# Softmax attention: three of four head pairs store their sums to DRAM and are normed later, with the head dims on partitions

## The chip, the cores and the metric

The kernel runs on one core of one Trainium2 chip. The metric is the device time of one execution in microseconds (us); the figure for a kernel is the median of its runs. A profile is one further execution, recorded by the hardware profiler.

## What is computed

A trunk of two layers over 1040 frames (16 learned meta frames and 1024 inputs) of 1024 features, in float32. Each layer norms its input, projects it, runs two head groups side by side (four heads of gated linear attention, GLA, and eight heads of softmax attention with a forget bias, FoX), norms each head, projects the concatenation back and adds it; then a gated feed-forward with a causal convolution. The part that matters here, cut from the reference:

```python
logits = jnp.einsum('bqhd,bkhd->bhqk', q_b, kf) + c_b[..., None] - c_k[:, :, None, :]
logits = jnp.where(key_pos[None, :] <= q_pos[:, None], logits, -jnp.inf)
o = jnp.einsum('bhqk,bkhd->bqhd', jax.nn.softmax(logits, axis=-1), vf)
...
o_fox = rms_norm(o_fox, fox_norm[i].reshape(FOX_HEADS, FOX_DH)).reshape(B, L, FOX_WIDTH)
h = h + jnp.concatenate([o_gla, o_fox], axis=-1) @ w_out[i]
```

A head has 64 dims. With s the unnormalised sum of exp(logit) v and z the sum of exp(logit), the softmax output is s / z, and its RMS norm is s / sqrt(mean(s^2) + EPS z^2): the denominator never divides, it only enters the norm as EPS z^2. Both kernels use this form (64 EPS z^2 beside the sum of squares over 64 dims).

## The kernel before, in words

Everything is kept with features on the 128 partitions and frames along the free dim. A float32 product is made of three passes in a faster float format: an operand is split into a rounded part and the rest, hi and lo, and `mm3` (L252 to L258) issues hi x hi, lo x hi and hi x lo. `split` (L369) makes the two parts with a cast on ScalarE (ACT, L372) and a subtraction on VectorE (DVE, L373).

In each layer the GLA heads run first, then the FoX stage (`fox`, L823), then the output projection and the feed-forward. The FoX stage treats the eight heads as four pairs p (two heads e of 64 dims fill 128 partitions) and the 1040 query frames as nine tiles of 116 frames (the first has 112), in five groups g of tiles: (7, 8), (5, 6), (3, 4), (1, 2), (0,). One step, or slot, is one tile of one head: 18 slots for a pair, 72 for a layer, eight more to drain.

A step n does the following, and a table `due` holds what follows in later slots:

- `fox_scores` (L697): two matmuls for each chunk of up to 464 keys into a PSUM tile of tag S (three buffers), bias and minimum on DVE (L715), the exponential on ACT (L727), which also sums the row; the row sums are gathered in `den` (L731), queries on partitions.
- slot n+2: the probabilities P are transposed on TensorE (PE, L748) and split into PT.
- slot n+3: `fox_av` (L752). PT is the moving operand; the stationary one holds V's hi part in 64 columns and its lo part in the other 64. So the result `av` (PSUM, one buffer) has the 64 head dims twice on the partitions, the sum with V hi and the sum with V lo, and the frames along the free dim. ACT copies it to SBUF (L777, `avs`).
- slot n+4, after head 1 of a group: `fox_fold` (L779). Four PE transposes (two for the single-tile group) turn `avs` so that frames lie on partitions (L787); ACT copies the hi part (L790), DVE adds the lo part (L791); ACT squares (L793), DVE sums over the 64 dims (L797), adds 64 EPS z^2 (L795, L798), and `rsqrt` (L305 to L311) gives a factor for each frame and head, tiles of a few elements a row; DVE multiplies (L802).
- slot n+6: `fox_store` (L806). Two transposes (one) bring the dims back on partitions (L813). Pairs 0, 1 and 2 are scaled by the norm's gain on ACT (L820) and stored by a DMA issued on GpSimd (POOL, L821) in a DRAM tensor `mixd`; pair 3 is split at once into the operand of the output projection (L817).

Between these, `work.run` fills every slot with projection matmuls ("mm" in the profile; 24 for a chunk of about 348 frames): while a pair is under way, the projections of the next pair (`fox_products`, L607) and then those of a GLA output gate (`gr_products`, L664). A gate unit is evacuated with single buffers of tags ge and gy and one of the two buffers of tag vt, in a chain of DVE and ACT operations (L672 to L683), and the gated GLA head goes to `mixd` as well. The last plan (L1028) loads the last parts of `mixd` (L1031, POOL), splits all of them into the operand of the output projection (L1047) and starts that projection inside the FoX stage.

The order of the instructions on each engine is made from program order by priority (the scores stand eight higher, L871) and by when their inputs are expected. SP (SyncE) issues the weight loads (L214), the moves of k (L638), the bias rows cb (L863) and the loads of GLA heads for the gates (L669), in one queue.

## Time and profile before

| | us |
|---|---|
| median of 3 runs (lowest to highest) | 2478.85 (2476.86 to 2479.68) |
| the profiled execution, device time | 2479.26 |
| its span in the trace | 2477.3 |
| mean granted TensorE clock of it | 0.997 |

| engine | share of the span busy |
|---|---|
| PE (matmuls) | 99% |
| DVE | 76% |
| ACT | 53% |
| POOL | 16% |

In the lines of the profile "L787" is line 787 of the kernel, "out<-in" are the program's names, sizes are partitions x elements, and times are us unless marked ns. PEld is the loading of PE's stationary operand, which overlaps the matmuls; the ends of matmuls are modelled. In a line of busy time by stretch the first figures are the stretch and its length, then each engine's busy time with its number of instructions, then the granted clock, the busy share of the DMA engines and GB/s. In a row of a source line stand the count, then the least, median and longest duration in ns, then the first and last start.

### The profile page before, as it was taken

Reading aid. Unit: us, or ns where it says so; the run is one execution under the profiler, and the core shown is the slowest. Engines: PE = TensorE matmul, PEld = TensorE weight load, DVE = VectorE, ACT = ScalarE, POOL = GpSimd, SP = SyncE. Lnnn points to the kernel's source line nnn. Section 1 sums busy time; section 2 is a strip of 40 time slices with the busy share of each in tenths; the row PEclk is TensorE's granted clock in tenths of the full one; section 3 lists DMA queues with packets and bytes.
Section 4 is the critical chain, followed back from the end, with each engine's and each line's share of the span. In section 5 each row is a group of like instructions: output and inputs, shape, how many; then the busy total and the mean of one; then the engine's idle time right before and its main releaser. Section 6 shows DMA issues by size and latency. Waiting matters only on the chain.

```text
span 2477.3 us, 47313 instructions
## 1 busy us (share of the span) xinstructions
PE 2447.8 (99%) x18286; PEld 2365.1 (95%) x18286; DVE 1875.6 (76%) x3769; ACT 1321.2 (53%) x2857; POOL 384.0 (16%) x565
## 2 busy tenths in 40 slices
PE   9999999999999999999999999999999999999998
PEld 8999999999999999999999999999999999998887
DVE  7666776869988888865865666777699888887667
ACT  7345766646555555642643466666465555556433
POOL 2023433210000000100210234331100000001002
PEclk9999999999999999999999999999999999999999
DMA  4232134333322214764412222243423212247722
GB/s 135 73 84 75 43 95 130 125 125 102 120 75 81 88 68 143 197 153 136 128 41 75 77 79 73 68 146 108 148 82 111 91 65 90 82 149 180 214 72 87
DMA packets 121872, 261.00 MB, mean 105 GB/s; under 512 B 15136, under 2 KB 36896, under 8 KB 121648
## 3 DMA queue, kind: packets, MB, share of 16 engines
q1 hardware_dynamic: 97440, 182.81, 23.9%
q0 software_dynamic: 22336, 72.88, 10.4%
q8 instruction: 143, 2.34, 0.4%
q10 hardware_dynamic: 1872, 2.31, 0.3%
q14 instruction: 81, 0.66, 0.1%
HBM read 177.31 MB, written 67.85 MB: 99 GB/s over the span
## 4 chain that ended last, share of the span: by engine, by line
PE 66%; issue 16%; DVE 11%; ACT 4%; DMA 2%; POOL 1%; SPq 0%; DVEq 0%; POOLq 0%; ACTq 0%
PE mm L256 8%; PE mm L258 7%; PE mm L257 7%; PE up L257 5%; PE up L258 5%; PE up L256 5%; PE down L257 4%; PE down L256 4%; PE down L258 4%; PE av L774 3%; PE tr L748 2%; PE S L712 1%; ACT P L727 1%; DVE S L715 1%; PE S L713 1%
## 5 line engine op out<-in xcount | busy, mean ns | idle before, releaser
L257 PE MATMUL up<-x,lo 128*128 128x260 f32 x2240 | 632.9, 283 | 0.9 <-DVE lo L1156 0.8
L256 PE MATMUL up<-x,hi 128*128 128x260 f32 x2240 | 632.8, 283 | 0.1
L258 PE MATMUL up<-x,hi 128*128 128x260 f32 x2240 | 632.9, 283 | 0.0
L257 PEld LDWEIGHTS up<-x,lo 128*128 128x128 f32 x2240 | 421.7, 188 | 1.4 <-DVE lo L1156 1.3
L256 PEld LDWEIGHTS up<-x,hi 128*128 128x128 f32 x2240 | 421.6, 188 | 0.4 <-ACT hi L1155 0.3
L258 PEld LDWEIGHTS up<-x,hi 128*128 128x128 f32 x2240 | 421.9, 188 | 0.0
L1155 ACT CAST hi<-raw 128x512 fp32r<-128x512 f32 (+1 forms) x490 | 266.4, 553 | 209.2 <-PE up L258 90.9
L256 PE MATMUL mm<-xh,hi 128*128 128x348 f32 (+4 forms) x1056 | 362.0, 343 | 0.0
L1156 DVE TENSOR_TENSOR lo<-raw,hi 128x512 fp32r<-128x512 f32 (+1 forms) x490 | 286.8, 600 | 78.7 <-ACT hi L1155 78.0
L258 PE MATMUL mm<-xl,hi 128*128 128x348 f32 (+4 forms) x1056 | 340.6, 322 | 0.0
L257 PE MATMUL mm<-xh,lo 128*128 128x348 f32 (+4 forms) x1056 | 339.7, 322 | 0.0
L256 PEld LDWEIGHTS mm<-xh,hi 128*128 128x128 f32 x1056 | 200.5, 190 | 2.0 <-issue 1.4
L257 PEld LDWEIGHTS mm<-xh,lo 128*128 128x128 f32 x1056 | 200.4, 190 | 0.1
L258 PEld LDWEIGHTS mm<-xl,hi 128*128 128x128 f32 x1056 | 199.2, 189 | 0.1
L1137 DVE TENSOR_TENSOR raw<-raw,raw 128x512 f32<-128x512 f32 (+1 forms) x230 | 147.0, 648 | 32.4 <-DMA raw<-in_wd_dram 30.1
L727 ACT ACTIVATE P<-S,m 116x460 f32<-116x460 f32 (+2 forms) x224 | 125.1, 562 | 71.5 <-DVE m L715 68.4
L256 PE MATMUL down<-x,hi 128*128 128x260 f32 (+1 forms) x504 | 161.1, 320 | 0.7 <-DVE dg L1614 0.7
L257 PE MATMUL down<-x,lo 128*128 128x260 f32 (+1 forms) x504 | 161.2, 320 | 0.4 <-DVE lo L1156 0.4
L223 ACT CAST hi<-raw 128x512 fp32r<-128x512 f32 (+2 forms) x152 | 87.4, 576 | 138.4 <-PE mm L258 53.8
L258 PE MATMUL down<-x,hi 128*128 128x260 f32 (+1 forms) x504 | 161.1, 320 | 0.0
L373 DVE TENSOR_TENSOR PT<-tr,PT 116x464 fp32r<-116x464 f32 (+3 forms) x240 | 122.9, 515 | 48.8 <-ACT PT L372 47.3
L1416 POOL DMA_DIRECT2D actd<-cv x44 | 23.5, 535 | 736.9 <-DVE cv L1415 736.9
(313 smaller groups left out, 5960.5 us busy)
## 6 DMA issues: line engine op xcount, KB each, us to landing
raw<-in_wm_dram SPq DMA_DIRECT2D x330, 256.0 KB, 3.0
raw<-in_wd_dram SPq DMA_DIRECT2D x48, 256.0 KB, 4.7
actd<-cv POOLq DMA_DIRECT2D x22, 520.0 KB, 3.0
actd<-cv POOLq DMA_DIRECT2D x22, 512.0 KB, 3.1
cb<-cd SPq DMA_DIRECT2D x16, 520.0 KB, 4.2
hm<-h POOLq DMA_DIRECT2D x32, 260.0 KB, 3.7
kA<-kA SPq DMA_DIRECT2D x24, 260.0 KB, 4.2
kL<-kL SPq DMA_DIRECT2D x24, 260.0 KB, 4.8
```

The costliest lines, as they stand in the source:

```text
L223: nc.scalar.copy(hi[:, :n, :], raw[:, :n, :])
L256: nc.tensor.matmul(ps, wh, xh[:, c0:c0 + n], start=first, stop=False, skip_group_check=more)
L257: nc.tensor.matmul(ps, wl, xh[:, c0:c0 + n], start=False, stop=False, skip_group_check=more)
L258: nc.tensor.matmul(ps, wh, xl[:, c0:c0 + n], start=False, stop=last, skip_group_check=more)
L373: nc.vector.tensor_tensor(out=lo, in0=src, in1=hi.bitcast(F32), op=ALU.subtract)
L712: nc.tensor.matmul(S[:rows, :n], q["qA"][e][:, qs], q["kA"][e][:, c0:k1], start=True, stop=False)
L727: nc.scalar.activation(P[:rows, :n], S[:rows, :n], AF.Exp, scale=-1.0, bias=m[:rows, nch - 1:nch], accum_out=(den if nch == 1 else d3[:row ...
L748: nc.tensor.transpose(tr[:w, 3 - j, :rows], P[:rows, o:o + w], id_)
L774: nc.tensor.matmul(av[:, a:b], w.rearrange("p a b -> p (a b)"), x, start=(t == ts[0] and part == 0 and i == 0), stop=(t == last and i == 1))
L1137: nc.vector.tensor_tensor(out=q[out][:, :nk, :], in0=q[a][:, :nk, :], in1=q[b][:, :nk, :], op=op)
L1155: nc.scalar.copy(hi[:, :nk, :], src[:, :nk, :])
L1156: nc.vector.tensor_tensor(out=lo[:, :nk, :], in0=src[:, :nk, :], in1=hi[:, :nk, :].bitcast(F32), op=ALU.subtract)
```

## The change

For pairs 0, 1 and 2 the fold, its norm and the store are taken out. Pair 3 keeps them.

- `fox_av`: the hi and lo sums are on different partitions of `av`; ACT copies one of the two halves (64 partitions) over to the other's partitions, DVE adds the other half from PSUM. Head 0 ends on partitions 0 to 63, head 1 on 64 to 127. After head 1, POOL issues the store of the unnormed sums in `mixd`.
- `fox_den`: twice for each pair (groups 0 to 2, groups 3 and 4) the row sums, squared and scaled, are turned by one PE transpose so that they lie as rows; SP stores the rows in a small DRAM tensor. The row sums of a pair now live in one tile for all nine tiles of queries.
- `fox_load`: in slot n+12, 10, 8, 6 or 6 (by group) SP loads the sums of the group back and, for each head, the row of 64 EPS z^2, repeated on 64 partitions.
- `fox_square`, at the end of that slot: squares on ACT, split into hi and lo.
- `fox_norm`, one slot later: two matmuls with a block matrix of ones (64 x 64 blocks on the diagonal, `pair`) sum the squares over each head's 64 dims and repeat the sum on its 64 partitions; DVE adds the denominators; `rsqrt` runs on the full width (128 partitions x 232 frames); DVE multiplies sums, gain and factor in one operation; POOL issues the store in `mixd`.

The working tiles of the new steps use the tags of others: ge, gy and vt of the gate units and projections, ff and fon of the fold. `avs` is used for the single-tile group too. The diff, cut to its core:

```diff
+        self.dd = [(dp.tile([12, FT], F32, name=f"dd{p}"), dp.tile([6, FT], F32, name=f"de{p}")) for p in range(3)]
...
-        if last < 4 * part + 4:
+        if last < 4 * part + 4 and to is None:
             nc.scalar.copy(avs[:, e, :width], av[:, :width])
+        elif last < 4 * part + 4:
+            own, oth = slice(64 * e, 64 * e + 64), slice(64 - 64 * e, 128 - 64 * e)
+            nc.scalar.copy(avs[own, 0, :width], av[oth, :width])
+            nc.vector.tensor_tensor(out=avs[own, 1, :width], in0=av[own, :width], in1=avs[own, 0, :width], op=ALU.add)
+            if e:
+                c0 = self.start_of(tiles[0])
+                nc.gpsimd.dma_start(to[:, c0:c0 + width], avs[:, 1, :width])
...
-        if mix is not None:
-            self.split(mix[0][:, c0:c0 + n], mix[1][:, c0:c0 + n], trf[:, :n], self.v(lyr, V_XN, p))
-            return
-        st = ap.tile([128, 2 * FT], F32, tag="fst", name="fst", bufs=1)
-        nc.scalar.mul(st[:, :n], trf[:, :n], self.v(lyr, V_XN, p))
-        nc.gpsimd.dma_start(self.mixd[4 + p][:, c0:c0 + n], st[:, :n])
+        self.split(mix[0][:, c0:c0 + n], mix[1][:, c0:c0 + n], trf[:, :n], self.v(lyr, V_XN, p))
+
+    def fox_den(self, p, r, den, ap, pp):
+        nc = self.nc
+        t0, n = ((3, 6), (0, 3))[r]
+        src = den[:FT, :, t0:t0 + n]
+        d2 = ap.tile([128, 12], F32, tag="fdp", name="fdp", bufs=2)[:FT, :2 * n]
+        nc.vector.scalar_tensor_tensor(out=d2.rearrange("p (a b) -> p a b", b=n), in0=src, scalar=64.0 * EPS, in1=src,
+                                       op0=ALU.mult, op1=ALU.mult)
+        tr = pp.tile([128, 4, 128], F32, tag="S", name="tr")
+        nc.tensor.transpose(tr[:2 * n, 0, :FT], d2, self.ident[:FT, :FT])
+        row = ap.tile([128, 256], F32, tag="fon", name="fr", bufs=1)[:2 * n, :FT]
+        nc.scalar.copy(row, tr[:2 * n, 0, :FT])
+        nc.sync.dma_start(self.dd[p][r][:], row)
+
+    def fox_load(self, p, g, tiles, st, ap):
+        nt, rows, c0 = len(tiles), self.rows_of(tiles[0]), self.start_of(tiles[0])
+        n = nt * rows
+        st["O"] = O = ap.tile([128, 2 * FT], F32, tag="fO", name="fO", bufs=1)[:, :n]
+        self.nc.sync.dma_start(O, self.mixd[4 + p][:, c0:c0 + n])
+        st["d2"] = d2 = ap.tile([128, 256], F32, tag="ff", name="fd2", bufs=1)[:, :n]
+        r = int(g > 2)
+        a = FT * (tiles[0] - (0 if r else 3))
+        x = self.dd[p][r][:].rearrange("(e t) r -> e (t r)", e=2)
+        for e in range(2):
+            self.nc.sync.dma_start(d2[64 * e:64 * e + 64], x[e:e + 1, a:a + n].to_broadcast([64, n]))
+
+    def fox_square(self, st, ap):
+        O = st["O"]
+        n = O.shape[1]
+        sq = ap.tile([128, 348], F32, tag="ge", name="fsq", bufs=1)[:, :n]
+        hi = ap.tile([128, 348], F32R, tag="gy", name="fsh", bufs=1)[:, :n]
+        lo = ap.tile([128, 348], F32R, tag="vt", name="fsl", bufs=self.vt_bufs)[:, :n]
+        self.nc.scalar.activation(sq, O, AF.Square)
+        self.split(hi, lo, sq)
+        st["sq"] = hi, lo
+
+    def fox_norm(self, lyr, p, tiles, st, ap, pp):
+        nc = self.nc
+        O = st["O"]
+        n = O.shape[1]
+        c0 = self.start_of(tiles[0])
+        ps = pp.tile([128, 512], F32, tag="S", name="fs")[:, :n]
+        for i, x in enumerate(st["sq"]):
+            nc.tensor.matmul(ps, self.pair[:], x, start=i == 0, stop=i == 1)
+        v, y0, a = (ap.tile([128, 348], F32, tag=t, name="fw", bufs=b)[:, :n]
+                    for t, b in (("ge", 1), ("gy", 1), ("vt", self.vt_bufs)))
+        nc.vector.tensor_tensor(out=v, in0=ps, in1=st["d2"], op=ALU.add)
+        self.rsqrt(y0, v, y0, a, scale=1.0 / 64)
+        nc.vector.scalar_tensor_tensor(out=v, in0=O, scalar=self.v(lyr, V_XN, p), in1=y0, op0=ALU.mult, op1=ALU.mult)
+        nc.gpsimd.dma_start(self.mixd[4 + p][:, c0:c0 + n], v)
...
-            for kind in ('av0', 'T0'):
+            for kind in ('den', 'load', 'av0', 'T0'):
...
             run(n, "fold")
+            run(n, "norm")
             for c in parts:
                 run(n, "av" + c)
                 run(n, "T" + c)
                 work.run(fill_us / (1 + len(parts)))
+            run(n, "square")
...
-        if e == 1:
+        if e == 1 and p == 3:
             at(n + 4, "fold", fold)
             at(n + 6, "store", store)
+        elif e == 1:
+            if g in (2, 4):
+                at(n + 2, "den", lambda: self.fox_den(p, int(g > 2), st["den"], ap, pp))
+            s0 = n + (12, 10, 8, 6, 6)[g]
+            at(s0, "load", lambda: self.fox_load(p, g, tiles, st, ap))
+            at(s0, "square", lambda: self.fox_square(st, ap))
+            at(s0 + 1, "norm", lambda: self.fox_norm(lyr, p, tiles, st, ap, pp))
```

More of the change, by code (lines that the diff above doesn't have):

```diff
@@ L750, in fox_transposes, with fox_av @@
         self.split(PT[ci][:w, 0, at, qs], PT[ci][:w, 1, at, qs], tr[:w, at, :rows])
-    def fox_av(self, e, tiles, q, PT, avs, pp, part):
+    def fox_av(self, e, tiles, q, PT, avs, pp, part, to):
         nc = self.nc
@@ L915, in f @@
                 if e == 0 and ci == 0:
-                    one = len(tiles) == 1
-                    st["avs"] = ap.tile([128, 2, FT if one else 2 * FT], F32, tag="av1" if one else "avs",
+                    one = p == 3 and len(tiles) == 1
+                    st["avs"] = ap.tile([128, 2, FT if one else 2 * FT], F32, tag="fO" if one else "avs",
                                         name="avs", bufs=1)
-                self.fox_av(e, tiles, q, PT, st["avs"], pp, ci)
+                self.fox_av(e, tiles, q, PT, st["avs"], pp, ci, None if p == 3 else self.mixd[4 + p])
             return f
@@ L1009, in attention @@
                 box = {}
+                self.pair = ap.tile([128, 128], F32R, tag="pair", name="pair", bufs=1)
+                for e in range(2):
+                    h, z = slice(64 * e, 64 * e + 64), slice(64 - 64 * e, 128 - 64 * e)
+                    nc.scalar.copy(self.pair[h, h], self.ones[h, h])
+                    nc.scalar.mul(self.pair[h, z], self.ones[h, z], 0.0)
                 KORD = (4, 5, 0, 1, 2, 3, 6)
```

18 lines of the change are left out of this document (12 added, 6 removed).

## The prediction

> **What bounds the kernel now.** I read the page first: the share of each engine, and the chain that ended last.
>
> ```profile
> span 2477.3 us, 47313 instructions
> PE 2447.8 (99%) x18286; PEld 2365.1 (95%) x18286; DVE 1875.6 (76%) x3769; ACT 1321.2 (53%) x2857; POOL 384.0 (16%) x565
> PE 66%; issue 16%; DVE 11%; ACT 4%; DMA 2%; POOL 1%; SPq 0%; DVEq 0%; POOLq 0%; ACTq 0%
> ```
>
> TensorE is busy for 99% of the span and carries most of the chain. So a TensorE instruction taken out is worth its issue time, unless the stretch it stood in has another limit. The change touches only the attention stages (about 170 to 480 us in layer 0, 1400 to 1735 us in layer 1), so I asked for busy time by stretch there (stretch, length, then PE, PEld, DVE, ACT and POOL).
>
> ```profile
> core 0: us, PE busy (x) PEld busy (x) DVE busy (x) ACT busy (x) POOL busy (x), PEclk, DMA share, GB/s
> 405.00:440.00 35.00, 34.85 (x240) 32.83 (x239) 30.49 (x97) 26.51 (x81) 10.00 (x20) 1.00 0.47 153
> 440.00:475.00 35.00, 31.62 (x234) 30.58 (x233) 33.42 (x101) 25.72 (x76) 10.45 (x20) 1.00 0.48 150
> 247.00:272.00 25.00, 24.86 (x170) 23.21 (x169) 22.94 (x75) 19.37 (x61) 7.81 (x12) 1.00 0.19 58
> 228.00:247.00 19.00, 19.00 (x138) 18.72 (x137) 9.85 (x34) 8.69 (x28) 5.88 (x9) 1.00 0.74 198
> 450.00:460.00 10.00, 7.04 (x59) 6.59 (x58) 9.87 (x34) 10.00 (x30) 1.66 (x3) 1.00 0.35 107
> 1680.00:1690.00 10.00, 8.48 (x59) 8.42 (x60) 9.87 (x33) 10.00 (x29) 2.11 (x4) 0.83 0.32 97
> ```
>
> Three kinds of stretch are to be seen. In most of the stage PE is full and DVE half empty (228 to 247). Where one head pair hands over to the next (247 to 272), PE is still full but DVE has only 25.00 - 22.94 = 2.06 us left: the gate units (gr) are evacuated there and the score rows are longest. And at the end, where the mixed outputs are split for the output projection (450 to 460; 1680 to 1690 in layer 1), ACT and DVE are full and PE stands still for 2.96 and 1.52 us. The chain in order of time says the same of that place:
>
> ```profile
> 454.64 1.64 ACT mh L372 x4
> 460.57 2.81 DVE ml L373 x6
> ```
>
> There a microsecond more on DVE or ACT is a microsecond more of time; everywhere else in the stage PE decides.
>
> **What comes off PE.** The timeline of PE shows one fold and what follows it, and a run of eight matmuls over 232 columns; the rows by source line give the counts.
>
> ```profile
> 200.22 0.32 PE L258 MATMUL mm<-xl,hi 128*128 128x348 f32 x1
> 200.38 0.60 PE L787 MATMUL fo<-ident,avs 128*116 128x128 f32 x4
> 200.81 0.36 PE L748 MATMUL tr<-ident,P 116*116 116x116 f32 x2
> 200.94 0.41 PE L256 MATMUL mm<-xh,hi 128*128 128x348 f32 x1
> 201.19 0.32 PE L257 MATMUL mm<-xh,lo 128*128 128x348 f32 x1
> 440.55 1.09 PE L774 MATMUL av<-PT,V 116*128 116x232 f32 x8
> 441.47 0.36 PE L748 MATMUL tr<-ident,P 116*116 116x116 f32 x2
> L787 PE MATMUL fo<-ident,avs x144: 270/272/323, 200.4 to 1730.1; 128*116 128x128 f32 x128, 128*112 128x128 f32 x16
> L813 PE MATMUL tr<-ident,fon x72: 259/262/267, 210.0 to 1734.7; 116*128 116x116 f32 x64, 112*128 112x112 f32 x8
> ```
>
> Matmuls overlap, so the price is the distance between starts, not the duration of about 270 ns: four fold transposes take 200.81 - 200.38 = 0.43 us, 0.107 us each. Three of four pairs lose theirs: 108 of the 144 in folds and 54 of the 72 in stores, 162 x 0.107 = 17.4 us. The first product after transposes starts its successor 0.25 us later (200.94 to 201.19) where the usual distance is 0.16 (200.22 to 200.38), so a block of transposes that stands alone costs 0.09 more. There are 60 such blocks (a fold and a store for each of 5 groups, 3 pairs, 2 layers), at most 5.4 us; next to the transposes of P (L748), as here, the turn is there anyway, and I take a third, 1.8. Off PE: 19.2 us, between 17.4 and 22.8.
>
> **What comes on PE.** Each group's norm is two matmuls of 232 columns against the block of ones. Eight of that size take 441.47 - 440.55 = 0.92 us, so 0.115 each; 24 groups of two tiles make 48, 5.5 us. Six single-tile groups make 12 of 112 columns, which I price as transposes, 1.3 us. The denominators take two transposes for each of 6 pairs, 12; half of them follow no other transposes and pay the turn: 12 x 0.107 + 6 x 0.09 = 1.8. On PE: 8.6 us. Net on PE: -10.6 us.
>
> **What moves on DVE.** These are the rows of a group before, and of a DVE operation at the width the new ones have.
>
> ```profile
> L791 DVE TENSOR_TENSOR ff<-fo,ff x40: 277/422/425, 201.7 to 1731.0; 116x256 f32<-116x256 f32 x32, 112x128 f32<-112x128 f32 x8
> L797 DVE TENSOR_REDUCE fv<-fon x40: 274/420/423, 202.8 to 1731.7; 116x4 f32<-116x256 f32 x32, 112x2 f32<-112x128 f32 x8
> L798 DVE TENSOR_TENSOR fv<-fv,fd x40: 146/158/593, 203.2 to 1732.2; 116x4 f32<-116x4 f32 x32, 112x2 f32<-112x2 f32 x8
> L802 DVE TENSOR_TENSOR fon<-ff,fy x72: 278/284/293, 204.9 to 1733.4; 116x128 f32<-116x128 f32 x64, 112x128 f32<-112x128 f32 x8
> L373 DVE TENSOR_TENSOR PT<-tr,PT 116x232 fp32r<-116x232 f32 x14 | 5.5, 393 | 2.9 <-ACT PT L372 2.7
> ```
>
> A two-tile fold is 0.42 + 0.42 + 2 x 0.284 and five tiny operations of 0.16 (L795, L798 and the three of the rsqrt, taken at L798's median): 2.2 us. A single-tile fold, at its minima, is 0.28 + 0.27 + 0.28 + 0.8 = 1.6. After, a two-tile group has two adds out of the sums' PSUM tile, one subtraction for the split, one add of the denominators, three operations of rsqrt and the last product, eight of 0.39: 3.1 us; a single-tile group eight of 0.27: 2.2. ACT trades five operations of a group (copy, square, two tiny, scale) for four (square, cast, Ln, Exp), so I count it as even.
>
> What matters is where they lie. The folds of groups 3 and 4 of the first pair and group 3 of the third give the clock:
>
> ```profile
> 252.16 0.60 PE L787 MATMUL fo<-ident,avs 128*116 128x128 f32 x4
> 262.08 0.43 PE L787 MATMUL fo<-ident,avs 128*112 128x128 f32 x2
> 415.48 0.60 PE L787 MATMUL fo<-ident,avs 128*116 128x128 f32 x4
> ```
>
> A pair has 18 slots, and these folds come at the end of slots 19, 21 and 55: a slot is 5 us there. The norms come in slots 16, 18, 20, 22 and 24, each with its split one slot before. In 247 to 272 there are then three two-tile norms (5 x 0.39 each, 5.9 us), splits of 0.39, 0.39 and 0.27, and 0.9 of sums, against 3.8 us of folds gone: 4.1 more where DVE has 2.06, an overhang of 2 us. It is handed to the stretch behind, and PE has the gate and projection units to run meanwhile; in 247 to 272 it lost 0.14 us with DVE at 92%. I take 0.3 us at each of the four hand-overs, 1.2 us; the bounds are 0 and 2 each. In 405 to 440 the same 4 us go into 4.5 that DVE has left. The norm of the single-tile group of the third pair, at the end of slot 60 (440.5), falls behind 440, where DVE sets the end: 5 x 0.27 = 1.35 us in each layer, 2.7 us, taken in full; the bounds are 0 (if the split of the mix still waits for the last gate unit) and twice that.
>
> One rule bears on DVE. This is the row of its one odd case, and what POOL did then:
>
> ```profile
> L681 DVE SCALAR_TENSOR_TENSOR gy<-ge,gy x12: 505/520/1450, 252.6 to 456.1; 128x348 f32<-128x348 f32 x8, 128x344 f32<-128x344 f32 x4
> 261.98 1.45 DVE L681 SCALAR_TENSOR_TENSOR gy<-ge,gy 128x348 f32<-128x348 f32 x1
> 261.77 1.28 POOL L225 TENSOR_TENSOR lo<-raw,hi 128x512 fp32r<-128x512 f32 x1
> ```
>
> The operation took 1.45 us instead of 0.52, and it ended 0.38 us after POOL's. The Trainium skill (SBUF — State Buffer, "Who interferes with whom") says that a VectorE instruction with two inputs in SBUF is blocked by a GpSimd instruction that reads SBUF until that one ends; the trace agrees here. By that rule the five wide operations of each norm with both inputs in SBUF would meet POOL at its 31% of 247 to 272, for half an operation of 1.3 us: as an estimate 5 x 0.2 = 1 us for each norm, and the sum would be that of the second rival below. I stay with the row's own rate, one blocked in 12 for 0.93 us, 0.4 us a norm, which lies inside the bounds above.
>
> **What is moved past the queues.** POOL gets five more DMA issues for each pair, SP fifteen loads and two stores of the denominator rows. Prices, and SP's neighbours at a hand-over (mean to landing last):
>
> ```profile
> mixd<-fst POOLq DMA_DIRECT2D x12, 116.0 KB, 3.3
> kL<-kL SPq DMA_DIRECT2D x9, 260.0 KB, 4.7
> L821 POOL DMA_DIRECT2D mixd<-fst x30: 555/562/565, 212.4 to 1666.4; - x30
> ```
>
> 30 x 0.56 us on POOL (7.81 of 25 busy) cost nothing by themselves. Sums are stored at slot n+3 and read back at n+6 or later, at least 12 us against 3.3, so the way through DRAM is covered. The loads stand behind kL and cb on SP; the square on ACT is due 4 to 5 us after its load, so a landing of 4.7 us is just covered, and if not, ACT waits and the exponentials of the scores behind it. Nothing taken; the bound is 1 us for each hand-over. The last piece of the third pair comes one slot later, some 5 us; its split (columns 0 to 400) runs at 460 and after, which covers it.
>
> **Sum.** The profiled execution took 2479.26 us, 1.96 more than its span and 0.41 above the median of the three runs. 2479.3 - 10.6 + 1.2 + 2.7 = 2472.6; I say 2472.5 us.
>
> **Rivals.** *DVE eats the gain (no change).* If the overhang at the four hand-overs reaches PE in full, 2479.3 - 10.6 + 8 + 2.7 = 2479.4; at half, 2475.4. For it: 92% of DVE there, and the 2.96 us that PE lost at 99%. Against it: PE lost 0.14 us at 92%, and DVE is half empty right before.
>
> *The shared buffers set the end (slower).* The norm borrows the single buffers ge and gy of the gate units. One gate unit holds them from its maximum to its last product:
>
> ```profile
> 422.01 0.34 DVE L675 TENSOR_SCALAR ge<-gx 128x348 f32<-128x348 f32 x1
> 426.45 0.51 DVE L683 SCALAR_TENSOR_TENSOR gog<-gy,gog 128x348 f32<-128x348 f32 x1
> 457.05 0.51 DVE L683 SCALAR_TENSOR_TENSOR h<-gy,gog 128x344 f32<-128x344 f32 x1
> 466.28 1.05 DVE L373 TENSOR_TENSOR ml<-h,mh 128x400 fp32r<-128x400 f32 x2
> ```
>
> That is 5 us. A norm holds them for about ten operations of 0.4 us and, as its result leaves from ge, until the store has landed, 3.3 us: 7.3 us. From the end of slot 53 to that of slot 62 (405 to 450) there are six gate units and four norms, 30 + 29 = 59 us for 45: 14 late. The last gate unit then ends not at 457.6 but at 471.6; its columns are split from 466.3 on, so a lag over 8.5 us decides, and 5.5 us of each layer are PE's: 2472.5 + 11 = 2483.5, and 2500.5 if nothing covers the lag. For it: gate units are dense just there, and PE already stops. Against it: ge is free between a square and its norm, and most holds overlap. At the other hand-overs (three units, four norms: 44 us in 38) the lag stays within one projection unit.
>
> *Off the path.* That the transposes were hidden anyway: PE at 99% speaks against it; the time would be 2479. It goes with the first rival.
>
> **Chances.** My forecast 0.47, DVE eating the gain or nothing happening 0.28, the shared buffers 0.25. A difference under 0.2% (5 us) can't be told from none here: faster (under 2473.9) 0.47, within 0.28, slower 0.25. The range goes from 2466 (22.8 off PE, no price at the hand-overs: 2479.3 - 14.2 + 1) to 2487, just past the price of the slower rival; about 0.05 lies below and 0.12 above.
>
> **What would show it.** PE should have 90 matmuls fewer (162 out, 72 in) and the hand-overs should stay 99% busy. The longest wait of PE in the stage, for the first split of the mix, should grow by little over a microsecond in each layer:
>
> ```profile
> PE mm L258 <- DVE ml L373: 1.8, 1, 1.8
> ```
> I am wrong if PE idles in 247 to 272, if DVE or ACT waits on landings of the new loads, or if the last gate unit's product (L683 into h) ends more than 8 us behind the last gate matmul compared with now.

## The result, and the profile after

The kernel after the change takes 2560.05 us (median of 5 runs, 2559.37 to 2565.9), the kernel before 2478.85 (5 runs, 2474.6 to 2479.68): a ratio of 1.0339, 95% interval 1.0328 to 1.0349, slower by 81 us where I had forecast 2472.5. The profiled execution took 2565.9 us, with a mean granted clock of 0.988 where it was 0.997.

First the page of the kernel after: the span, the engines' shares and the chain that ended last.

```profile
span 2564.1 us, 47602 instructions
PE 2469.1 (96%) x18196; PEld 2371.3 (92%) x18196; DVE 1908.2 (74%) x3757; ACT 1337.5 (52%) x2847; POOL 403.3 (16%) x601
issue 14%; PE 11%; DVE 5%; DMA 1%; ACT 1%; POOL 0%; SPq 0%; DVEq 0%; POOLq 0%; ACTq 0%
```

PE has 90 matmuls fewer, as forecast, and DVE and ACT are no fuller than before (74% and 52%, from 76% and 53%). No engine took PE's place as the bound: PE has less to do and stands still more. (Its busy time in us is longer all the same, in part because its clock is lower in places, as the next rows show.)

Where it stands still, the busy time by stretch tells (stretch, length, then PE, PEld, DVE, ACT, POOL, granted clock), over 300 us of layer 0, before and then after.

```profile
230.00:290.00 60.00, 59.86 (x423) 57.64 (x422) 44.71 (x145) 39.65 (x123) 20.06 (x30) 1.00 0.33 92
290.00:350.00 60.00, 59.80 (x420) 57.55 (x418) 40.50 (x131) 37.95 (x118) 22.86 (x32) 1.00 0.31 93
350.00:410.00 60.00, 59.90 (x431) 58.91 (x431) 36.92 (x117) 35.77 (x107) 24.72 (x35) 1.00 0.34 100
410.00:470.00 60.00, 56.48 (x401) 53.63 (x400) 55.42 (x170) 47.45 (x140) 16.91 (x33) 1.00 0.40 124
470.00:530.00 60.00, 60.00 (x438) 59.63 (x437) 34.28 (x98) 23.03 (x68) 5.17 (x11) 1.00 0.32 105
```

```profile
230.00:290.00 60.00, 53.77 (x340) 50.56 (x339) 42.16 (x124) 34.88 (x101) 16.86 (x26) 0.91 0.34 100
290.00:350.00 60.00, 53.79 (x358) 51.45 (x357) 35.13 (x102) 33.15 (x101) 24.48 (x35) 0.96 0.34 93
350.00:410.00 60.00, 54.32 (x357) 51.18 (x356) 41.97 (x118) 37.26 (x100) 22.18 (x32) 0.96 0.19 60
410.00:470.00 60.00, 52.50 (x349) 49.88 (x349) 37.37 (x112) 33.02 (x97) 17.52 (x29) 0.94 0.48 144
470.00:530.00 60.00, 52.81 (x358) 48.52 (x357) 52.16 (x158) 40.81 (x118) 15.07 (x29) 1.00 0.41 125
```

Idle time of PE: 300 - 296.04 = 3.96 us before, 300 - 267.19 = 32.81 after, 28.9 more. The clock, at 0.91, 0.96, 0.96 and 0.94 in four rows of 60 us, is worth up to (0.09 + 0.04 + 0.04 + 0.06) x 60 = 13.8 more; up to, because some of the slow time is idle time already. Together that is up to 42.7 us in these 300. What the whole layer lost is read between markers, two DMA issues on SP: the first bias row (cb) of the second pair and the first load after the stage (h), in the timeline before and after:

```profile
238.86 0.33 SPq L863 DMA_DIRECT2D cb<-cd  x1
466.98 5.04 SPq L1069 DMA_DIRECT2D h<-in_hT_dram  x3
```

```profile
237.12 0.33 SPq L917 DMA_DIRECT2D cb<-cd  x1
509.92 3.21 SPq L1143 DMA_DIRECT2D h<-in_hT_dram  x3
```

The first marker comes 1.74 us earlier: 16 of the first pair's transposes are gone ahead of it (1.7 us at the prediction's price), and no product of a norm has run yet (the first starts at 239.1). The rest of the stage is (509.92 - 237.12) - (466.98 - 238.86) = 44.7 us longer, so layer 0 lost 42.9, near the sum above. In layer 1 the stretch between the same two markers is 47.3 us longer (1467.81 to 1695.90 before, 1506.05 to 1781.48 after). With what lies between the two stretches, 4.7 us shorter, and behind them, 1.2 longer, that makes the 86.8 us by which the span grew.

What PE waits for, over the whole span (total, times, longest), and for how long ACT sat idle before the squares until the norm's store had landed (total, times):

```profile
PE fs L869 <- ACT P L728: 28.9, 6, 7.0
PE fs L869 <- ACT fsh L373: 18.5, 15, 2.1
```

```profile
  DMA mixd<-fw: 30.7, 10
```

fs is the new product of the squares. It waits for an exponential because it takes one of the three PSUM tiles (tag S) in which the scores stand until ACT has read them. The first of the six long waits, in the timelines of DVE, POOL, SP, ACT and PE:

```profile
243.64 0.45 DVE L874 SCALAR_TENSOR_TENSOR fw<-fO,vec,fw 128x232 f32<-128x232 f32 x1
249.05 0.40 DVE L374 TENSOR_TENSOR fsl<-fsq,fsh 128x232 fp32r<-128x232 f32 x1 [2.33 <-ACT fsh L373]
249.37 0.34 DVE L716 CUSTOM_DVE_ANT_0 S<-S,cb,m 116x116 f32<-116x116 f32 x1
244.38 0.56 POOL L875 DMA_DIRECT2D mixd<-fw  x1 [1.19 <-DVE fw L874]
244.11 0.76 SPq L844 DMA_DIRECT2D fO<-mixd  x1
248.20 0.40 ACT L858 ACTIVATE fsq<-fO 128x232 f32<-128x232 f32 x1 [3.49 <-DMA mixd<-fw]
249.80 0.64 ACT L728 ACTIVATE P<-S,m 116x460 f32<-116x460 f32 x1 [0.78 <-DVE m L716]
246.58 0.49 PE L646 MATMUL tr<-ident,vt 128*116 128x128 f32 x3
250.58 0.56 PE L869 MATMUL fs<-fsh,pair 128*128 128x232 f32 x1 [3.52 <-ACT P L728]
```

DVE ends a norm, and POOL issues its store from ge at 244.38. The next group's squares go to the same ge, so ACT stands before them until the store has landed, 3.82 us, at 248.20. The next sums are loaded in the same time (SP at 244.11, right after the last reader of the single buffer fO). DVE stands as well, 2.33 us, before the low parts of these squares (249.05), and behind them in its order is the reduce of the last chunk of scores (249.37). The exponentials stand behind the squares in ACT's order and then wait 0.78 us more for that reduce; they begin at 249.80, the score tile comes free, and PE goes on at 250.58. The clock of the same place, in stretches of 2 us:

```profile
248.00:250.00 2.00, 0.00 (x0) 0.00 (x0) 0.95 (x4) 0.98 (x3) 0.44 (x2) 0.83 0.16 59
250.00:252.00 2.00, 1.42 (x4) 1.03 (x5) 0.94 (x4) 2.00 (x9) 0.00 (x0) 0.50 0.00 0
254.00:256.00 2.00, 2.00 (x9) 2.00 (x8) 2.00 (x7) 1.49 (x5) 0.77 (x1) 0.50 0.00 0
258.00:260.00 2.00, 2.00 (x17) 1.87 (x16) 1.83 (x6) 0.79 (x2) 0.37 (x1) 1.00 0.55 133
```

After the wait of 3.5 us PE gets half its clock for some 6 us (9 matmuls in 254 to 256, 17 in 258 to 260). So this stall costs its own length and about 3 us more, half of the 6.

### The profile page after: what moved, and what is told of

It reads as the page before. It is cut to its first block, busy times and chain, and to the rows that moved or that the text cites. A ratio compares the mean times of both kernels' runs of the same rounds, so it can differ in the third digit from the quotient of the medians.

```text
span 2564.1 us, 47602 instructions
## 1 busy us (share of the span) xinstructions
PE 2469.1 (96%) x18196; PEld 2371.3 (92%) x18196; DVE 1908.2 (74%) x3757; ACT 1337.5 (52%) x2847; POOL 403.3 (16%) x601
## 5 line engine op out<-in xcount | busy, mean ns | idle before, releaser
L373 ACT CAST PT<-tr 116x464 fp32r<-116x464 f32 (+3 forms) x240 | 107.0, 449 | 90.5 <-PE tr L749 81.7
L728 ACT ACTIVATE P<-S,m 116x460 f32<-116x460 f32 (+2 forms) x224 | 125.0, 561 | 45.4 <-DVE m L716 42.5
```

What stands on the lines that cost most here:

```text
L373: nc.scalar.copy(hi, src)
L728: nc.scalar.activation(P[:rows, :n], S[:rows, :n], AF.Exp, scale=-1.0, bias=m[:rows, nch - 1:nch], accum_out=(den if nch == 1 else d3[:row ...
```

## The experiments

Theory 1: the buffer ge, held until the norm's store has landed, makes ACT wait, and the exponentials with it; in a wide form, all buffers shared with the gate units. Theory 2: the sums come back late through DRAM and the single buffer fO. Theory 3: the added steps of DVE and ACT delay the scores' own steps by themselves. The others are named where they came up. Each kernel was run once beside a run of the kernel before on the same chip. Those runs of before lie between 2473.93 and 2479.83, so I compare by the difference from them and rest nothing on less than 6 us. The choice matters where a gap is small: avs_sp is 9.1 us under fs_tr by the differences and 6.0 by the times themselves. Two things change along with the edits and were not tried by themselves. The order of the instructions is made anew for each kernel; from 251 to 253 us, for one, PE takes scores ahead of four transposes in no_norm and the transposes first in chain_no_pe. And from own4 on the mask is in BF16 (POOL's step with it has a median of 0.41 us in two_two and of 0.44 in the kernel after). L numbers move by one or two in some of these kernels.

| run | us | before beside it | difference |
|---|---|---|---|
| no_norm | 2470.52 | 2479.83 | -9.3 |
| v_fon | 2537.49 | 2479.83 | +57.7 |
| o_two | 2564.01 | 2479.83 | +84.2 |
| own4 | 2545.81 | 2479.83 | +66.0 |
| fix_O | 2534.57 | 2476.40 | +58.2 |
| two_two | 2525.33 | 2476.40 | +48.9 |
| early | 2529.33 | 2476.40 | +52.9 |
| early_late | 2535.76 | 2476.40 | +59.4 |
| fs_tr | 2516.39 | 2473.93 | +42.5 |
| late_slots | 2543.12 | 2473.93 | +69.2 |
| hi_only | 2521.32 | 2473.93 | +47.4 |
| all3 | 2531.05 | 2473.93 | +57.1 |
| dma_only | 2480.79 | 2476.97 | +3.8 |
| compute_only | 2518.80 | 2476.97 | +41.8 |
| pe_only | 2473.76 | 2476.97 | -3.2 |
| avs_sp | 2510.37 | 2476.97 | +33.4 |
| chain_no_pe | 2513.11 | 2478.67 | +34.4 |
| own_chain | 2511.62 | 2478.67 | +33.0 |

**no_norm.** Is the loss in the norms at all?

```diff
-            at(s0, "load", lambda: self.fox_load(p, g, tiles, st, ap))
-            at(s0, "square", lambda: self.fox_square(st, ap))
-            at(s0 + 1, "norm", lambda: self.fox_norm(lyr, p, tiles, st, ap, pp))
```

> Left out: the loading back of the sums, their squares and their norm, for the first three pairs (the denominators are still stored as rows); the sums go to the output projection unnormed. All theories that put the loss in the norm steps expect the PE sum alone: 19.2 us off PE less 1.8 for the denominators, 2479 - 17 = 2462, with at most 2 us of waits. A loss that sits in the sums themselves (the copy and add out of PSUM, the single-buffer avs, the store on GpSimd) or in the denominators would leave it over 2490.

It measured 2470.52 us (-9.3), between the two expectations. The loss goes with the three steps left out, but about 8 us of the saving that was expected on PE did not come.

**v_fon, o_two, own4.** One suspected buffer at a time, then all those of the gate chain.

```diff
# v_fon: the norm's result leaves from fon, not from ge
-                    for t, b in (("ge", 1), ("gy", 1), ("vt", self.vt_bufs)))
+                    for t, b in (("fon", 1), ("gy", 1), ("vt", self.vt_bufs)))
# o_two: the loaded sums alternate between two buffers
-        st["O"] = O = ap.tile([128, 2 * FT], F32, tag="fO", name="fO", bufs=1)[:, :n]
+        st["O"] = O = ap.tile([128, 256 if g % 2 else 2 * FT], F32, tag="fon" if g % 2 else "fO", name="fO", bufs=1)[:, :n]
# own4: squares in vt, hi and y0 in fon, lo and a in a new tag fsl, the result over d2
+        sq = ap.tile([128, 348], F32, tag="vt", name="fsq", bufs=self.vt_bufs)[:, :n]
+        hi = ap.tile([128, 256], F32R, tag="fon", name="fsh", bufs=1)[:, :n]
+        lo = ap.tile([128, 2 * FT], F32R, tag="fsl", name="fsl", bufs=1)[:, :n]
...
+        v = st["d2"]
+        y0 = ap.tile([128, 256], F32, tag="fon", name="fw", bufs=1)[:, :n]
+        a = ap.tile([128, 2 * FT], F32, tag="fsl", name="fw", bufs=1)[:, :n]
-        self.mask = c.tile([128, 128], F32, name="mask")
+        self.mask = c.tile([128, 128], BF16, name="mask")
```

> The norm's result goes to the buffer fon (free of the fold in these pairs) instead of ge; all else as in the changed kernel. Theory 1 (the shared buffer ge is held until the norm's store has landed, the next square waits for it on ACT, and the exponentials stand behind it): the 30.7 us in which ACT waits for the landing of the store go, and with them about as much of PE's standing and the dip of the clock after it: 30 to 45 us faster than the changed kernel, 2515 to 2530. Theory 2 (the sums come back late through DRAM and the single buffer fO): no change, 2560. Theory 3 (the added DVE and ACT work itself): no change, 2560.

> The sums that are loaded back alternate between two buffers (fO and fon), so the next load needn't wait for the last use of the one before; ge stays shared. Theory 1: within 8 us of the changed kernel, 2552 to 2565, and ACT still waits about 30 us for the landing of stores. Theory 2: 30 us or more faster, 2530 or less, and the waits of ACT for landings go.

> The norm uses no buffer of the gate units any more: squares in one of the two vt buffers for a moment, hi and the first factor in fon, lo and the helper in a new buffer of 232 columns, the norm's result in the buffer of the denominators. To make room the triangular mask is bf16. Theory 1 in its wide form (the stalls are all waits for ge and gy, for a landing or for a gate unit's chain): 2470 to 2490. If only the landing counts: like v_fon, 2515 to 2530. Theory 3 (the work itself on DVE and ACT): over 2530.

v_fon took 81.2 - 57.7 = 23.5 us off the kernel after, where theory 1 wanted 30 to 45: ge's wait for the store is real, but it is not most of the loss. What came next shows in ACT's waits of v_fon:

```profile
ACT fsq L858 <- DMA fO<-mixd: 38.6, 18, 4.0
```

The squares now wait for the loaded sums. o_two alone gained nothing. That the wait for ge and the wait for fO hid behind each other fits this, but o_two's trace does not show it: ACT stands idle before the squares for 27.5 us (5 times) without a releaser that the profile names, and only for 2.8 us until a store has landed. own4, free of ge and gy, was no better than v_fon; but its squares, too, wait for the loaded sums (27.8 us, 18 times), so it does not settle theory 1 in its wide form.

**fix_O, two_two, early, early_late.** Take the landing out altogether, or bring it forward.

```diff
# fix_O: v in fon as in v_fon; squares, denominators and last product read a constant tile
-        self.nc.scalar.activation(sq, O, AF.Square)
+        self.nc.scalar.activation(sq, self.fix[:, :n], AF.Square)
# two_two (mask in BF16 to make room)
+        st["O"] = O = ap.tile([128, 2 * FT], F32, tag="fO", name="fO", bufs=2)[:, :n]
...
+        st["d2"] = d2 = ap.tile([128, 256], F32, tag="fon" if g % 2 else "ff", name="fd2", bufs=1)[:, :n]
...
+        v = st["d2"]
+        y0, a = (ap.tile([128, 348], F32, tag=t, name="fw", bufs=b)[:, :n]
+                 for t, b in (("gy", 1), ("vt", self.vt_bufs)))
# early = two_two and
+            at(s0 - 1, "load", lambda: self.fox_load(p, g, tiles, st, ap))
# early_late = early and
+            at(s0 + 1 + (p < 2), "norm", lambda: self.fox_norm(lyr, p, tiles, st, ap, pp))
```

> The norm's result goes to a buffer of its own (as in v_fon), and the squares, the addition of the denominators and the last product read a constant tile in place of what was loaded back; loads and stores are still issued, so the output of three pairs is not the norm of their sums. Nothing on ACT, PE or DVE waits for a landing any more, and all the work of the norms is there. Theory 2 (the sums come back late): 2470 to 2490 us, near the 2470.52 without the norms. Theory 1 alone (only the buffer ge that waits for the store): no gain over the 2537.49 of v_fon, 2530 to 2540. Theory 3 (the added work on DVE and ACT itself): 2515 or more.

> Two buffers for the sums loaded back, two for the denominators, the norm's result written over the denominators; ge is used for the squares alone, nothing else moved. The loads no longer wait for the norm of the group before, but are still issued in the slot in which the squares stand. Theory 2, if the single buffer is what makes the sums late: 2475 to 2505 us. Theory 2, if the trip itself (2 to 4 us from issue to landing in a slot of 4.5) makes them late: 2515 to 2540, as v_fon. Theory 3: 2530 to 2545.

> As two_two, and the loads are issued one slot (about 4.5 us) earlier, the squares and the norm where they were. Theory 2: the wait of ACT for the landing goes, 2472 to 2500 us. Theory 3 and theory 1 in its wide form (the waits for ge and gy shared with the gate units stay): 2515 to 2540.

> As early, and for the first two pairs the norm (its matmul first) stands one slot later, a whole slot behind the squares. If what is left in early is PE standing in order before the matmul of squares whose rounding ACT or DVE has not done, this takes most of it: 5 to 20 us under early. If what is left is the added work (theory 3), or the waits for ge: within 4 us of early.

two_two gains 8.7 us on v_fon, which by its range would leave the blame with the trip itself. But in its trace the trip is hardly waited for any more; this is what ACT sat idle for at the tiles fsq, whole span, and what PE waited for in 230 to 530:

```profile
  DMA fO<-mixd: 2.5, 6
```

```profile
PE S L713 <- ACT P L728: 8.1, 6, 2.4
PE fs L869 <- ACT P L728: 4.2, 3, 1.6
```

And fix_O, in which nothing of the norm reads what is loaded, still stands at +58.2, no better than v_fon. It is not free of landings, as was expected: its result leaves from the single buffer fon, and DVE sat idle before the tiles fw, over the whole span, until that store had landed:

```profile
  DMA mixd<-fw: 11.2, 6
```

In two_two that wait is gone, too, and two_two is 9.3 us faster than fix_O. So theory 2 falls as the main cause, and it stays open how much of the last 9 us belongs to the late sums and how much to the result's buffer. Loading a slot earlier (early) gave nothing, and the later norm (early_late), which was to take 5 to 20 us off or change nothing, cost 6 us more.

**fs_tr, late_slots, hi_only, all3.** A place, a time and a quantity.

```diff
# fs_tr = two_two and
-        ps = pp.tile([128, 512], F32, tag="S", name="fs")[:, :n]
+        ps = pp.tile([128, 4, 128], F32, tag="tr", name="fs")[:].rearrange("p a b -> p (a b)")[:, :n]
# late_slots = two_two and
-            s0 = n + (12, 10, 8, 6, 6)[g]
+            s0 = n + (12, 10, 8, 6, 6)[g] if p == 2 else 18 * p + 25 + 2 * g
# hi_only = two_two and (one matmul in place of two)
-        self.nc.scalar.activation(sq, O, AF.Square)
-        self.split(hi, lo, sq)
-        st["sq"] = hi, lo
+        self.nc.scalar.activation(hi, O, AF.Square)
+        st["sq"] = hi,
```

> As two_two, and the product of squares goes to the PSUM tiles of the transposes instead of the score tiles. fix_O showed that landings are not what is left; in two_two PE waits 4.2 us (3 times) before this product and 8.1 us (6 times) before scores for a score tile that an exponential on ACT has to free, in 300 us of layer 0. Theory 4 (the product takes one of three score tiles away just when they are all in use): most of these waits go, 2495 to 2510 us from 2525.33. Theory 3 (the added DVE and ACT work stands ahead of the reduces and exponentials, wherever the product goes): 2518 to 2530.

> As two_two, and the squares and norms of the first two pairs stand in slots 7 to 16 of the next pair, past the four slots of three score chunks; pair 3 of 4 as before. Theory 5 (the steps were put where a slot has most reduces and exponentials; elsewhere DVE and ACT have room): 2495 to 2510 us. Theory 3 (the work costs the same anywhere): 2520 to 2530.

> As two_two, with the squares rounded once and their low parts left out: per group one cast, one subtraction of 0.4 to 0.95 us and one matmul fewer. PE's own part, 30 matmuls at 0.26 us, is 8 us; theory 3 (it is the quantity of added DVE and ACT work that counts): 2500 to 2512 us. Theory 4 or 5: only PE's part and a little, 2514 to 2520.

> The three edits together. If they take separate waits, the sum of their gains: 2470 to 2490 us, at or under the kernel before the change if the prediction's saving on PE was there. If all three take the same waits, no better than the best of them.

fs_tr gained 6.4 us where theory 4 wanted 15 to 30. That does not clear the score tiles: PE's wait for an exponential before fs (8.7 us over the whole span of two_two) is gone, but one of 8.5 us has come up before the denominators' transpose (L835), which takes a score tile as well and is not among PE's waits in two_two. hi_only gained nothing that one run can show (1.5), though it has two of ten steps of ACT and DVE and 30 products fewer: the quantity alone does not set the price. late_slots lost 20, but not by its idea alone: two of its waits in 413 to 503, one of PE and one of DVE, show a new stall, the norm's addition standing for denominators that were loaded late.

```profile
PE S L713 <- DVE fd L873: 9.4, 1, 9.4
```

```profile
DVE fd L873 <- DMA fd<-dd: 4.4, 1, 4.4
```

So theory 5 stays undecided. all3, at +57.1, carries the same move. fs_tr showed one more shared thing, in the timelines of POOL and ACT:

```profile
420.64 0.55 POOL L876 DMA_DIRECT2D mixd<-fd  x1
421.56 0.56 POOL L785 DMA_DIRECT2D mixd<-avs  x1
427.69 0.25 ACT L781 COPY avs<-av 64x112 f32<-64x112 f32 x1 [2.64 <-DMA mixd<-avs]
```

The store of the sums stands on POOL's queue behind the norm's store, and avs has one buffer; ACT waits for it, 6.1 us after its issue.

**dma_only, compute_only, pe_only, avs_sp.** The norm's parts alone.

```diff
# dma_only = two_two without squares and norm; what was loaded is stored back
+        nc.gpsimd.dma_start(self.mixd[4 + p][:, c0:c0 + n], O)
# compute_only = fix_O without "load" and without the norm's store
# pe_only = no_norm and, where the norm stood,
+        for i in range(2):
+            nc.tensor.matmul(ps, self.pair[:], self.fix[:, :n], start=i == 0, stop=i == 1)
# avs_sp = fs_tr and, for the sums
-                nc.gpsimd.dma_start(to[:, c0:c0 + width], avs[:, 1, :width])
+                nc.sync.dma_start(to[:, c0:c0 + width], avs[:, 1, :width])
```

> The three pairs' loads (in the buffers of two_two) and stores alone: what was loaded is stored back unchanged; squares, products and norms are left out. Theory 6 (the transfers on the in-order queues of SP and GpSimd, and what stands behind them, are most of the 55 us by which two_two is over the 2470.52 of no_norm): 2500 to 2525 us. Theory 7 (the chain of ACT, PE and DVE itself, each in its order, is most of it): 2470 to 2482.

> The squares, products and norms on a constant tile, with no load and no store for them, so three pairs keep their sums as they are; the result in a buffer that no transfer holds. Theory 6: 2480 to 2495 us, PE's own part and little more. Theory 7: 2510 to 2530.

> no_norm and the 60 products with the pair matrix alone, on a constant, read by nothing, into the score tiles. Both theories: PE's own 60 products at 0.16 (the distance of neighbouring products) to 0.26 us (measured from start to start in two_two), 2480 to 2487. Over 2490: the score tile taken away, or PE's switch between shapes, is itself a large part.

> fs_tr, and the store of the sums on the queue of SP instead of GpSimd, where it stands behind the norm's store (which waits for DVE) and the four loads for the mix. Theory 6: ACT's waits for that store (2.6 us in the last pair) go, 2495 to 2510 us from 2516.39. Theory 7: 2512 to 2520. If SP's loads behind it wait for the sums instead, slower than 2520.

Over no_norm (-9.3) the transfers alone cost 13.1 us, PE's products alone 6.1, and the arithmetic chain with the products 51.1: theory 7. The parts nearly add up to two_two, which has them all: 13.1 + 51.1 = 64 against 58.2; on top of the chain the transfers cost less than alone, 7.1 us (two_two over compute_only). pe_only is faster than the 2480 to 2487 us that both theories gave it. avs_sp took 9.1 us off fs_tr: the store's queue was part of the transfers' price. In its waits over the whole span the denominators' transpose stands as it did in fs_tr:

```profile
PE tr L835 <- ACT P L728: 7.9, 6, 1.9
```

**chain_no_pe, own_chain.** What in the chain costs.

```diff
# chain_no_pe = compute_only and
-        for i, x in enumerate(st["sq"]):
-            nc.tensor.matmul(ps, self.pair[:], x, start=i == 0, stop=i == 1)
+        ps = st["sq"][1].bitcast(F32)
# own_chain = compute_only and
+        sq = ap.tile([128, 2 * FT], F32, tag="fO", name="fsq", bufs=1)[:, :n]
+        hi = ap.tile([128, 256], F32R, tag="ff", name="fsh", bufs=1)[:, :n]
+        lo = ap.tile([128, 256], F32R, tag="fon", name="fsl", bufs=1)[:, :n]
...
+        v = ap.tile([128, 2 * FT], F32, tag="fO", name="fw", bufs=1)[:, :n]
+        y0 = ap.tile([128, 256], F32, tag="ff", name="fw", bufs=1)[:, :n]
+        a = ap.tile([128, 256], F32, tag="fon", name="fw", bufs=1)[:, :n]
```

> compute_only without the product on PE: the denominators' addition reads the rounded-off parts instead of the product, everything else of ACT's and DVE's chain stays, so no norm is computed. compute_only took 2518.8 us where no_norm takes 2470.52. Theory 8 (PE, which works in order, stands before the product, because all three score tiles are in use or the squares are not yet rounded; the scores and exponentials behind it come late in turn): 2472 to 2488. Theory 3 (eleven steps on ACT and DVE that stand in their order ahead of reduces and exponentials are enough by themselves): 2500 to 2516.

> compute_only with none of the gate chain's buffers: squares, rounded parts, v, y0 and a lie in the three tiles that the loads, the denominators and the fold used. Theory 1 in its wide form (norm and gate chain hold each other up through ge, gy and vt): 2485 to 2502. Theory 8 or theory 3: 2510 to 2522.

Without PE's product the chain still costs 34.4 + 9.3 = 43.7 us, without the gate chain's buffers 42.3, against 51.1 with both. By the ranges set beforehand both runs fall to theory 3. Theories 8 and 1 (wide) get 7 to 9 us each, little more than one run can show, and theory 3 the rest by elimination, though by hi_only not in proportion to the steps. How a step of DVE does it shows at one place, the same in no_norm and in chain_no_pe: the first scores after a pair's hand-over, in the timelines of PE, DVE, ACT and PE, no_norm first (for chain_no_pe also POOL).

```profile
242.82 0.42 PE L713 MATMUL S<-kA,qA 128*116 128x460 f32 x1
243.83 0.65 DVE L716 CUSTOM_DVE_ANT_0 S<-S,cb 116x460 f32<-116x460 f32 x1
246.10 0.65 ACT L728 ACTIVATE P<-S,m 116x460 f32<-116x460 f32 x1 [2.42 <-DVE m L716]
246.89 0.26 PE L835 MATMUL tr<-ident,fdp 116*6 116x116 f32 x1
247.52 0.47 PE L713 MATMUL S<-kA,qA 128*116 128x460 f32 x1 [0.30 <-ACT P L728]
```

```profile
242.79 0.42 PE L713 MATMUL S<-kA,qA 128*116 128x460 f32 x1
242.34 1.49 POOL L226 TENSOR_TENSOR lo<-raw,hi 128x512 fp32r<-128x512 f32 x1 [0.21 <-ACT hi L224]
242.87 1.22 DVE L870 TENSOR_TENSOR fw<-fsl,fix 128x232 f32<-128x232 f32 x1
244.82 0.65 DVE L716 CUSTOM_DVE_ANT_0 S<-S,cb 116x460 f32<-116x460 f32 x1
247.10 0.64 ACT L728 ACTIVATE P<-S,m 116x460 f32<-116x460 f32 x1 [3.15 <-DVE m L716]
247.89 0.26 PE L835 MATMUL tr<-ident,fdp 116*6 116x116 f32 x1 [1.05 <-ACT P L728]
248.51 0.47 PE L713 MATMUL S<-kA,qA 128*116 128x460 f32 x1 [0.30 <-ACT P L728]
```

The scores are issued within 0.03 us of each other. In chain_no_pe the norm's addition stands on DVE ahead of the reduce, held up by POOL (more on that below); the reduce starts 0.99 us later and the exponential 1.00 later. PE stands idle for it, 1.05 us, before the denominators' transpose, which needs a score tile and did not wait in no_norm; its next scores come 0.99 later. So at this place a microsecond on DVE is a microsecond for PE, although DVE's busy share is no more than 83% (49.75 of 60 us in 230 to 290 of chain_no_pe). In 242 to 244, where the addition stands, DVE is full.

## Why the prediction was wrong

**The saving on PE** came true as work, and to about a third as time. The count of 90 matmuls was right, and so, in one profile of each kernel, was the sum: PE is busy for 2447.8 us before and for 2437.8 in pe_only, which has the transposes out and the products in but no norm, 10.0 us less where the sum had 10.6. In no_norm, without the products, it is 2432.6, 15.2 less where the sum had 17 (19.2 less 1.8 for the denominators' transposes). (Waits lengthen the busy time, if anything: compute_only has the matmuls and the mean clock of pe_only, 0.998, and is busy for 2455.3.) But PE also stands still longer: 29.5 us before, 34.2 in pe_only, 36.2 in no_norm. So in time pe_only stands at -3.2 us and no_norm at -9.3. What came with the sums and the denominators thus has a price that the prediction put at nothing, some 5 to 7 us of waits; they were not followed to their cause.

**The step that failed first** is "Nothing taken; the bound is 1 us for each hand-over", for what is moved past the queues. The text names the very wait, "if not, ACT waits and the exponentials of the scores behind it", and gives it no price. It compared one landing (4.7 us at most) with the slot, and did not put the two that follow each other in a row: the load cannot be issued before the norm before it is done with fO, nor the squares begin before that norm's store has left ge. Buffers and landings, from the kernel after (+81.2) to two_two (+48.9), are 32 us; the transfers that are left cost another 7 (on top of the chain) to 13 (alone).

**The second**, and the larger, is the overhang of DVE, "0.3 us at each of the four hand-overs, 1.2 us", with the reason that "PE has the gate and projection units to run meanwhile". The chain without transfers and without PE's product costs 43.7 us, in 30 norms 1.5 each. The price was looked for in DVE's free time (92% in 247 to 272), and over the stage DVE never was full: after the change it is busy for 42.16 of 60 us in 230 to 290. The traces point to who stands behind a step. The scores' reduce, the exponential and the split of P are a chain with PE at both ends, and PE's units to run meanwhile stand in its order too: in the place traced in the kernel after it stood for 3.52 us before the product, and the next projection matmul came behind the product and the scores, at 253.69. The counts of operations (3.1 us of DVE for a group against 2.2) were about right, and DVE's total hardly moved (1875.6 to 1908.2 us), so the quantity alone does not explain it. That it is the place in the order is argued from the one place traced above; no run moved the same steps to where they cost nothing.

**The rivals.** DVE eating the gain was taken as a limit of throughput, worth 8 us at most; as a delay, if the argument above holds, it is the largest term. The shared buffers had the mechanism, ge held until the store has landed, 3.3 us by the forecast and 3.82 at the place traced (2.5 from issue to landing, by the median of 24 such stores); but it was given weight only at the end of the stage, beside gate units. It acts at every hand-over, from norm to norm ("ge is free between a square and its norm" is true and beside the point: the store holds it from one norm to the next square), and at the place traced what it stops is ACT, and by that the exponentials. The gate units come late as well, as the third of the tests below shows; what that cost was not separated.

**The rule of the Trainium skill** (SBUF — State Buffer, "Who interferes with whom"), weighed in the prediction, is borne out once more by the lines of chain_no_pe: the addition, which there has both inputs in SBUF (in the kernel after, one is in PSUM), took 1.22 us instead of 0.39 and ended 0.26 us after POOL's subtraction. In the kernel after the same subtraction meets another step of the norm, in the timelines of POOL and DVE:

```profile
241.83 1.36 POOL L226 TENSOR_TENSOR lo<-raw,hi 128x512 fp32r<-128x512 f32 x1
242.38 1.06 DVE L312 SCALAR_TENSOR_TENSOR fw<-fw 128x232 f32<-128x232 f32 x1
```

Over all norms it is the smaller part, and an upper bound, since not every long step was looked up beside POOL: in chain_no_pe the six wide steps of DVE, by their means, take 18 us more than they would at 0.39 us each (0.45 for the last product), of the chain's 43.7. In the kernel after, the three steps of the norm whose means the profile lists (L310, L312, L874) take 0.41, 0.50 and 0.45 us, some 3 us more in all. I had priced it at 0.4 us a norm, 12 in all, and put it inside bounds that the sum then used at 1.2.

**The tests that were set** all three came out against the forecast: PE idles in 247 to 272 (20.84 of 25 us busy), ACT waits on landings of the new transfers, and the last gate unit's product starts 21.6 us behind the last gate matmul (484.49 to 506.06) where it was 8.8 before (448.29 to 457.05), 12.8 later. The wait of PE for the first split of the mix, which was to grow, is not among PE's waits any more.

What stays open: which of the chain's steps cost most (only one of them was followed to PE), how much of the differences is the order of instructions that each kernel got anew, and whether there are slots where the norms would cost nothing. No version that beats the kernel before was found; the best with the whole change is avs_sp, at +33.4.

## What to carry to other kernels

An engine that is 75% busy is not free: ask of each added step what stands behind it in its engine's order, and whether the engine that sets the time waits for that. Taking one wait away can show nothing (o_two) or only the next one (v_fon, fs_tr); running each part alone (transfers, products, arithmetic) told in three runs where the time was. And a buffer from which a store leaves was held here until the store had landed (ACT's 30.7 us before the squares), so its next user's place in its engine's order has to be that much later.

## What the runs showed of the hardware

The clock is the part I had not counted on: after 3.5 us without a matmul PE ran at 0.50 for about 6 us, and in layer 0 the lower clock made up to 13.8 of the 42.9 us lost. The Trainium skill (TensorE: Matmul & The Clock Gate, "HAM oscillation — how this bites in real kernels") asks for no idle gaps of PE over about 3.4 us; this place agrees. But a shorter gap was enough too. In the kernel after PE waits 2.01 us before a product, and the clock falls just the same, in stretches of 2 us:

```profile
282.00:284.00 2.00, 0.93 (x4) 0.74 (x5) 0.88 (x3) 0.38 (x1) 0.54 (x1) 0.86 0.35 108
284.00:286.00 2.00, 2.00 (x9) 1.81 (x8) 1.68 (x6) 1.05 (x3) 0.00 (x0) 0.50 0.19 70
```

Nor is the length of the gap all that decides. In the kernel before, PE waits for the first split of the mix once in each layer, 1.75 us up to 452.60 and 1.76 us up to 1681.52. Behind the first the clock stays at 1.00; behind the second it is 0.50 in 1684 to 1686. What else decides is not shown here. No run kept PE busy through a stall, so the clock's share was not tried by itself.
